# A hybrid encoder block on one core: Quarter 0's weight loads among the gate merges, T4 with the other sums, and a regrouped last quarter

## The chip, the core and the metric

The kernel runs on one core of a Trainium2 chip. Five engines matter: TensorE (PE; its weight loads are listed as PEld), VectorE (DVE), ScalarE (ACT), GpSimd (POOL) and SyncE (SP), which issues most of the DMAs. Each engine works through its own list of instructions in order and waits on semaphores. The metric is the device time of one execution in microseconds (us); less is better.

## The reference, cut to what matters

```
proj = u @ w_in                      # q, k, v of two attentions, and the gate logits
mix = (sigmoid(g_a) * (o_a @ w_branch_a) + sigmoid(g_b) * (o_b @ w_branch_b)) @ w_out
x = LN1(alpha * x + mix)
x = LN2(alpha * x + relu(x @ w_ff1)^2 @ w_ff2)      # w_ff1 1024x4096, w_ff2 4096x1024
```

There are 512 rows of 1024 columns, all in float32. Every large product is made of three matmuls on operands that were split into a rounded high part and a low remainder (line 84 makes the high part on ACT, line 85 the low part on DVE).

## The kernel before, in words

The work is laid out so that PE always has the next product. Weights of the first stages come as chunks of 512 KB (`raw`, loaded on line 126, three buffers), are split into `wh` and `wl`, and are used by `chunk()`. A tile framework puts each engine's instructions in an order of its own at build time; the engines then keep to it.

**The gate merges.** `branch(1, ...)` (line 597) makes the second branch's product in eight blocks. Each block is merged: DVE multiplies the bank by the gate (line 610), POOL adds the other branch (line 613), ACT rounds the result into `X` (line 615), DVE makes the remainder (line 616). The sixteen `G` buffers hold the gates until then.

**The output projection and LN1.** Two `s_group` loops follow (lines 916 and 934): 512 columns each, four row blocks, with the eight merged tiles against four weight chunks. The first takes its chunks as they come, the second has all four split beforehand into `V` tiles. After the second, each row block is normalised (`ln1`) and transposed on PE (line 801).

**The MLP.** Four quarters of 1024 hidden columns. `t_pair` makes the hidden tiles, ACT and DVE square and combine them. The product with a quarter of `w_ff2` is a 2x2 Strassen-Winograd scheme over row halves and column halves: seven products P1 to P7 instead of eight. Its right operands are made from four raw blocks per i (B11, B12, B22, B21, in `G` buffers of 256 KB, line 881): `sums` makes T1 = B12-B11, T3 = B22-B12, T2 = B22-T1 on DVE (line 823), and `prepare(n, i)` splits the operand of Pn. T4 is made in `prepare(6)`. B11 is loaded again after P7's operand was split, for P1, and B22 after P5's, for P3.

W and Z gather P7 and P5 over all quarters in four PSUM banks (`mm`). U gathers P1+P6 over all quarters in SBUF. `add_to` adds a bank or U to the residual rows x0 to x3 (lines 951 and 953). In the last quarter W, Z and U are added, then for b = 0 and 1 the products P4, P2 and P3 finish row blocks b+2 and b, `row_stats` (line 961) takes their statistics, and `layer_norm` (lines 728 to 742) writes them. The very last row block, 1, makes P3 in two halves of 256 columns and has a normalisation of its own, `layer_norm_last` (lines 751 to 775). Both halves of this P3 stand in one PSUM bank, `X2`:

```
X, Y, X2 = ([mm_bank()] * 2 for _ in range(3))          # line 1067
...
for lo, hi in ((0, 256), (256, S)) if b == LAST_ROW else ((0, S),):
    qt.run(3, X2, (b,), cuts=((lo, hi),))
    add_to(b, 1, X2[b][:, lo:hi], lo, hi)
    row_stats(b, 1, lo, hi)
```

Of the kernel before, what the change touches and what calls it, by code (L numbers as in the profile page):

```python
# [16 lines left out]
P = 128  # L17
# [23 lines left out]
def block_kernel(ctx, tc, w, w2, x_t, x, pos, relb, bgate, lq1, lk1, lq2, lk2, subg,  # L41
# [667 lines left out]
    for _ in branch(1, ob_h, ob_l):  # L709
        pass  # L710
# [105 lines left out]

    def sub(out, a, b):
        V.tensor_tensor(out=out, in0=a, in1=b, op=ALU.subtract)  # L823

    LEFT = {1: "A11", 2: "A12", 3: "S4", 4: "A22", 5: "S1", 6: "S2", 7: "S3"}
    lo_rows, hi_rows = slice(0, 256), slice(256, S)

    class Quarter:


        def __init__(self, q):
            self.q = q
            self.ops = {n: [None] * 4 for n in range(1, 8)}
            self.a = {}
            self.raw = [[self.load(i, r, c) for r, c in ((0, 0), (0, 1), (1, 1), (1, 0))]
                        for i in range(4)]
            self.ops[7] = [(vt(), vt()) for _ in range(4)]

        def left_tiles(self):
            for key in ("S3", "S1", "A11"):  # L840
                for i in (0, 2):
                    pair = (vt(), vt()) if key != "A11" else tuple(
                        late.tile([P, S], FR, tag="a11", bufs=4, name=name("a11"))
                        for _ in range(2))
                    for j in range(2):
                        self.a[key, i + j] = tuple(t[:, 256 * j:256 * (j + 1)] for t in pair)


        def square(self, ps):
            t = tmp_tile()  # L850
            A.activation(t, ps, AF.Relu)
            A.activation(t, t, AF.Square)
            return t

        def first(self, i):
            def f(ps):
                t = self.t0 = self.square(ps)
                sub(t[:, hi_rows], t[:, lo_rows], t[:, hi_rows])
                split(t[:, hi_rows], *self.a["S3", i])
                split(t[:, lo_rows], *self.a["A11", i])  # L860
            return f

        def second(self, i):
            def f(ps):
                t, t0, s1 = self.square(ps), self.t0, tmp_tile()[:, lo_rows]
                for left, right in (("A12", "A22"), ("S4", "S2")):
                    h, l = xt(FR), xt(FR)
                    split(t, h, l)
                    self.a[left, i] = h[:, lo_rows], l[:, lo_rows]
                    self.a[right, i] = h[:, hi_rows], l[:, hi_rows]  # L870
                    if left == "A12":
                        sub(t[:, hi_rows], t[:, hi_rows], t0[:, hi_rows])
                        V.tensor_tensor(out=s1, in0=t[:, hi_rows], in1=t0[:, lo_rows], op=ALU.add)
                        split(s1, *self.a["S1", i])
                        sub(t[:, lo_rows], t[:, lo_rows], t[:, hi_rows])
            return f


        def load(self, i, r, c, t=None):
            t = t or gt()  # L880
            nc.sync.dma_start(out=t, in_=w2[self.q, i, r, :, c * S:(c + 1) * S])
            return t

        def sums(self, i):
            b11, b12, b22, b21 = self.raw[i]
            sub(b11, b12, b11)
            sub(b12, b22, b12)
            sub(b22, b22, b11)

        def prepare(self, n, i, parts=None):  # L890

            b11, b12, b22, b21 = self.raw[i]
            src = {1: b12, 2: b21, 3: b11, 4: b22, 5: b11, 6: b22, 7: b12}[n]
            self.ops[n][i] = self.ops[n][i] or parts or (vt(), vt())
            split(src, *self.ops[n][i])
            if n == 7:
                self.load(i, 0, 0, b12)
            if n == 5:
                self.load(i, 1, 1, b11)
            if n == 6:  # L900
                sub(b22, b21, b22)

        def run(self, n, ps, blocks=(0, 1), first=True, stop=True, cuts=((0, S),)):
            jobs = [(b, lo, hi) for b in blocks for lo, hi in cuts]
            order = [(j, i) for i in range(4) for j in jobs] if n == 7 else \
                [(j, i) for j in jobs for i in range(4)]
            for (b, lo, hi), i in order:
                ah, al = (t[:, b * P:(b + 1) * P] for t in self.a[LEFT[n], i])
                wh, wl = (t[:, lo:hi] for t in self.ops[n][i])
                smm(ps[b][:, lo:hi], ah, al, wh, wl, first and i == 0, stop and i == 3)  # L910

# [3 lines left out]
    qt = None  # L915
    for n, _ in enumerate(s_group(mh, ml, evac_res(0))):
        prefetch(c0 + 5, min(c0 + 4, next_chunk[0] + 3))
        if n == 0:
            qt = Quarter(0)
        if n in (2, 4):  # L920
            for i in (n - 2, n - 1):
                qt.sums(i)
                qt.prepare(7, i)
# [39 lines left out]
    def first_pair(evacs):  # L963
        ch = [chunk() for _ in range(2)]
        ps2 = [mm_bank() for _ in range(2)]
# [13 lines left out]
    def store_row(s):  # L979
        def store(cols):  # L980
            q = A if cols.start in (S, 832) else nc.sync
            q.dma_start(out=out[s * P:(s + 1) * P, cols], in_=x1[s][:, cols])
        return store
# [3 lines left out]

    for q in range(4):
        last = q == 3
        qt.left_tiles()  # L990
# [6 lines left out]
        for i in range(4):  # L997
# [9 lines left out]
            prepare(5, (i,))  # L1007

# [7 lines left out]
        ends = dict(first=q == 0, stop=last)  # L1016
        qt.run(7, W, **ends)
        prepare(1)
        if last:
            for b in range(2):  # L1020
                add_to(b + 2, 1, W[b])
                add_to(b + 2, 0, W[b])
        qt.run(5, Z, **ends)
        prepare(6)
        if last:
            prepare(3, parts=(p3h, p3l))
            for b in range(2):
                add_to(b + 2, 1, Z[b])
                add_to(b, 1, Z[b])
# [3 lines left out]
        for b in range(2):  # L1033
            if q == 0:
                A.copy(out=U[b], in_=X[b])
            else:
                V.tensor_tensor(out=U[b], in0=U[b], in1=X[b], op=ALU.add)
            add_to(b, 0, X[b])
# [5 lines left out]
        if not last:  # L1044
# [3 lines left out]
            following = Quarter(q + 1)  # L1048
            for b in range(2):
                add_to(b, 0, X[b])  # L1050
            for i in range(4):
                following.sums(i)
                following.prepare(7, i)
# [11 lines left out]

        for b in range(2):
            X, Y, X2 = ([mm_bank()] * 2 for _ in range(3))
            for s, nh in ((b + 2, 0), (b + 2, 1), (b, 1)):
                add_to(s, nh, U[b])
            row_stats(b + 2, 1)  # L1070
            qt.run(4, X, (b,))
# [6 lines left out]
            for lo, hi in ((0, 256), (256, S)) if b == LAST_ROW else ((0, S),):  # L1078
                qt.run(3, X2, (b,), cuts=((lo, hi),))
                add_to(b, 1, X2[b][:, lo:hi], lo, hi)  # L1080
# [75 lines left out]
```

## Time and profile before

| | |
|---|---|
| median of 3 runs | 724.19 us (723.75 to 724.66) |
| the profiled execution | 725.08 us |
| its span, first to last instruction | 721.9 us |
| PE busy | 700.4 us, 97%, 3259 matmuls |
| DVE busy | 535.1 us, 74% |
| ACT busy | 382.1 us, 53% |
| POOL busy | 101.3 us, 14% |

The span is the time between the first and the last instruction of the program; 3.2 us of the profiled execution lie around it. Durations below come from this one execution. PE is at work nearly always, so a change can save time only where PE stands still or after PE's last matmul.

### The profile page before, as it was taken

What the parts mean: (1) busy time and instruction counts of PE and PEld (TensorE: products, weight loads), DVE (VectorE), ACT (ScalarE), POOL (GpSimd) and SP (SyncE); (2) the same over time, 40 slices, a digit from 0 to 9 for tenths busy, and PEclk for the clock granted to TensorE, in tenths of its full rate; (3) what the DMA queues carried; (4) which work ended last, traced back from release to release, by engine and by line L of the source; (5) the groups of instructions that cost most, each with busy time, mean ns of one, the idle gap of its engine ahead of it and who ended that gap; (6) DMA issues with size and microseconds to landing.
All of it is one profiled execution on the core that took longest, in us unless ns stands there. A gap on an engine that the chain in (4) does not pass through costs nothing.

```text
span 721.9 us, 9483 instructions
## 1 busy us (share of the span) xinstructions
PE 700.4 (97%) x3259; PEld 583.0 (81%) x3259; DVE 535.1 (74%) x1014; ACT 382.1 (53%) x698; POOL 101.3 (14%) x107
## 2 busy tenths in 40 slices
PE   9999999999999999999999999999999999999991
PEld 7888888888888888888788888888888888888881
DVE  6567668775667677759896899566984689465996
ACT  5556556645667666324366574266525674266500
POOL 2022266840121120043000000000000000000001
PEclk9999999999999999999999999999999999999996
DMA  8554233332332222376541336243451354222002
GB/s 295 197 160 127 90 85 88 103 107 73 116 109 68 67 81 88 107 277 206 197 147 65 103 125 198 94 146 117 143 178 59 124 167 160 75 88 76 12 30 87
DMA packets 36815, 87.27 MB, mean 121 GB/s; under 512 B 5664, under 2 KB 6432, under 8 KB 36768
## 3 DMA queue, kind: packets, MB, share of 16 engines
q1 hardware_dynamic: 35904, 85.56, 36.5%
q10 hardware_dynamic: 864, 1.11, 0.4%
q8 instruction: 25, 0.41, 0.2%
q14 instruction: 22, 0.18, 0.1%
HBM read 79.84 MB, written 2.10 MB: 114 GB/s over the span
## 4 chain that ended last, share of the span: by engine, by line
PE 84%; DVE 9%; ACT 2%; POOL 2%; issue 2%; DMA 0%; DVEq 0%
PE mm L184 9%; PE mm L186 9%; PE mm L185 9%; PE st L185 6%; PE st L184 6%; PE st L186 6%; PE st L189 4%; PE st L191 4%; PE st L190 4%; PE mm L189 4%; PE mm L190 4%; PE mm L191 4%; PE o L184 2%; POOL G L613 2%; PE o L185 2%; PE o L186 2%
## 5 line engine op out<-in xcount | busy, mean ns | idle before, releaser
L85 DVE TENSOR_TENSOR wl<-raw,wh 128x1024 fp32r<-128x1024 f32 (+1 forms) x86 | 105.0, 1222 | 33.2 <-ACT wh L84 33.1
L84 ACT CAST wh<-raw 128x1024 fp32r<-128x1024 f32 (+1 forms) x86 | 88.5, 1029 | 68.3 <-PE mm L185 24.1
L184 PE MATMUL mm<-X,wh 128*128 128x512 f32 x256 | 103.2, 403 | 0.0
L186 PE MATMUL mm<-X,wl 128*128 128x512 f32 x256 | 99.9, 390 | 0.0
L185 PE MATMUL mm<-X,wh 128*128 128x512 f32 x256 | 99.8, 390 | 0.0
L84 ACT CAST V<-G 128x512 fp32r<-128x512 f32 x108 | 63.7, 619 | 50.7 <-DVE G L823 25.3
L186 PE MATMUL st<-x1t,wl 128*128 128x512 f32 (+1 forms) x200 | 76.1, 381 | 0.0
L185 PE MATMUL st<-x1t,wh 128*128 128x512 f32 (+1 forms) x200 | 76.1, 381 | 0.0
L184 PE MATMUL st<-x1t,wh 128*128 128x512 f32 (+1 forms) x200 | 75.9, 381 | 0.0
L85 DVE TENSOR_TENSOR V<-G,V 128x512 fp32r<-128x512 f32 x108 | 73.8, 684 | 1.4 <-ACT V L84 1.4
L186 PEld LDWEIGHTS mm<-X,wl 128*128 128x128 f32 x256 | 48.0, 188 | 10.6
L184 PEld LDWEIGHTS mm<-X,wh 128*128 128x128 f32 x256 | 48.1, 188 | 8.8
L185 PEld LDWEIGHTS mm<-X,wh 128*128 128x128 f32 x256 | 48.2, 188 | 8.6
L285 ACT ACTIVATE e<-e,s 128x128 f32<-128x128 f32 (+3 forms) x64 | 36.0, 562 | 35.4 <-DVE s L283 34.7
L767 POOL TENSOR_SCALAR s<-s 128x1 f32<-128x1 f32 x1 | 0.4, 412 | 377.8 <-DVE s L751 377.8
L823 DVE TENSOR_TENSOR G<-G,G 128x512 f32<-128x512 f32 x64 | 46.1, 731 | 0.1
L378 POOL TENSOR_SCALAR e<-e,s 128x128 f32<-128x128 f32 (+3 forms) x32 | 36.8, 1149 | 66.3 <-DVE s L287 62.5
L191 PE MATMUL st<-V,X 128*128 128x512 f32 x116 | 45.0, 389 | 0.0
L190 PE MATMUL st<-V,X 128*128 128x512 f32 x116 | 44.9, 389 | 0.0
L189 PE MATMUL st<-V,X 128*128 128x512 f32 x116 | 44.8, 391 | 0.0
L185 PEld LDWEIGHTS st<-x1t,wh 128*128 128x128 f32 x200 | 37.6, 188 | 7.1
L186 PEld LDWEIGHTS st<-x1t,wl 128*128 128x128 f32 x200 | 37.6, 188 | 7.1
(255 smaller groups left out, 1573.5 us busy)
## 6 DMA issues: line engine op xcount, KB each, us to landing
raw<-in_w_dram SPq DMA_DIRECT2D x86, 512.0 KB
G<-in_w_dram SPq DMA_DIRECT2D x96, 256.0 KB
q<-q SPq DMA_DIRECT2D x32, 128.0 KB
G<-in_relb_dram SPq DMA_DIRECT2D x8, 256.0 KB
x<-in_x_dram SPq DMA_DIRECT2D x4, 512.0 KB
e<-in_x_t_dram SPq DMA_DIRECT2D x7, 256.0 KB
raw<-in_w_dram SPq DMA_DIRECT2D x4, 256.0 KB
out_dram<-x SPq DMA_DIRECT2D x3, 256.0 KB
```

The source lines that it names most:

```text
L84: A.copy(out=h, in_=src)
L85: i = (eng or V).tensor_tensor(out=l, in0=src, in1=h.bitcast(F32), op=ALU.subtract)
L184: T.matmul(ps, lw_h, rh, start=first, stop=False)
L185: T.matmul(ps, lw_h, rl, start=False, stop=False)
L186: T.matmul(ps, lw_l, rh, start=False, stop=last)
L189: T.matmul(ps, ah, w_h, start=first, stop=False)
L190: T.matmul(ps, ah, w_l, start=False, stop=False)
L191: T.matmul(ps, al, w_h, start=False, stop=last)
L285: A.activation(e[:, :n], e[:, :n], AF.Exp, bias=nm, scale=-1.0, accum_out=sums)
L378: G.tensor_scalar(ex[:, :n], ex[:, :n], r, None, op0=ALU.mult)
L613: G.tensor_tensor(out=m, in0=m, in1=g, op=ALU.add)
L823: V.tensor_tensor(out=out, in0=a, in1=b, op=ALU.subtract)
```

## The change

- `load_next`: the sixteen loads of Quarter 0's raw blocks are issued two at a time in the loop over `branch(1, ...)`, one pair for each merge, instead of at the first step of the first `s_group`. The other quarters load their sixteen at once, as before.
- `sums` now splits P7's operand itself and then makes T4 = B21-T2 into T3's buffer. So `prepare(7)` reloads nothing any more; B11 is loaded again after P5's split, B22 after P6's.
- Quarter 0's `sums` run at the first three steps of the first `s_group` and, for i = 3, in `first_pair`, instead of in pairs at steps 2 and 4.
- Last quarter: U of the first three quarters is added to six half rows (`flush(U)`) after the first hidden tile; P1's result is then copied to U by ACT, not added by DVE. W is no longer added by itself, but as U+W (`both`) to two half rows of each b. P1's operands are split ahead of P7 into spare `raw` and `wh` buffers. The last row's two P3 halves get a bank each. One store of the last row goes from ACT's queue to SP's.

```diff
+    qt = Quarter(0)
+    for n, _ in enumerate(branch(1, ob_h, ob_l)):
+        qt.load_next(2)
...
         def sums(self, i):
             b11, b12, b22, b21 = self.raw[i]
             sub(b11, b12, b11)
             sub(b12, b22, b12)
             sub(b22, b22, b11)
+            self.prepare(7, i)
+            sub(b12, b21, b22)
 
         def prepare(self, n, i, parts=None):
             b11, b12, b22, b21 = self.raw[i]
-            src = {1: b12, 2: b21, 3: b11, 4: b22, 5: b11, 6: b22, 7: b12}[n]
+            src = {1: b11, 2: b21, 3: b22, 4: b12, 5: b11, 6: b22, 7: b12}[n]
             self.ops[n][i] = self.ops[n][i] or parts or (vt(), vt())
             split(src, *self.ops[n][i])
-            if n == 7:
-                self.load(i, 0, 0, b12)
             if n == 5:
-                self.load(i, 1, 1, b11)
+                self.load(i, 0, 0, b11)
             if n == 6:
-                sub(b22, b21, b22)
+                self.load(i, 1, 1, b22)
...
         prefetch(c0 + 5, min(c0 + 4, next_chunk[0] + 3))
-        if n == 0:
-            qt = Quarter(0)
-        if n in (2, 4):
-            for i in (n - 2, n - 1):
-                qt.sums(i)
-                qt.prepare(7, i)
+        if n < 3:
+            qt.sums(n)
...
         ch = [chunk() for _ in range(2)]
+        qt.sums(3)
...
-            q = A if cols.start in (S, 832) else nc.sync
+            q = A if cols.start == (832 if s == LAST_ROW else S) else nc.sync
...
+    def flush(u, rows=((2, 0), (2, 1), (0, 1))):
+        for b in range(2):
+            for s, nh in rows:
+                add_to(b + s, nh, u[b])
...
             prepare(5, (i,))
+            if last and i == 0:
+                flush(U)
...
+        if last:
+            for i in range(0, 4, 2):
+                parts = [wp.tile([P, 1024], FR, tag=t, bufs=3, name=name(t))
+                         for t in (("raw", "raw"), ("raw", "wh"))[i // 2]]
+                for j in range(2):
+                    qt.prepare(1, i + j, [t[:, 512 * j:512 * (j + 1)] for t in parts])
         qt.run(7, W, **ends)
-        prepare(1)
-        if last:
-            for b in range(2):
-                add_to(b + 2, 1, W[b])
-                add_to(b + 2, 0, W[b])
+        if not last:
+            prepare(1)
...
-            if q == 0:
+            if q == 0 or last:
                 A.copy(out=U[b], in_=X[b])
...
+        both = [tmp_tile() for _ in range(2)]
         for b in range(2):
-            X, Y, X2 = ([mm_bank()] * 2 for _ in range(3))
-            for s, nh in ((b + 2, 0), (b + 2, 1), (b, 1)):
-                add_to(s, nh, U[b])
+            V.tensor_tensor(out=both[b], in0=U[b], in1=W[b], op=ALU.add)
+            for s, nh, t in ((b + 2, 0, both), (b + 2, 1, both), (b, 1, U)):
+                add_to(s, nh, t[b])
             row_stats(b + 2, 1)
+            X, Y = ([mm_bank()] * 2 for _ in range(2))
...
             for lo, hi in ((0, 256), (256, S)) if b == LAST_ROW else ((0, S),):
-                qt.run(3, X2, (b,), cuts=((lo, hi),))
-                add_to(b, 1, X2[b][:, lo:hi], lo, hi)
+                X = [mm_bank()] * 2
+                qt.run(3, X, (b,), cuts=((lo, hi),))
+                add_to(b, 1, X[b][:, lo:hi], lo, hi)
```

**How it moves instructions: the last quarter, DVE, from P6's first bank on.** `u` is U, `o` and `st` are PSUM banks, `x_2` is row block 2, `bn` its statistics, `lt` is `both`, `V` are split operands. Before:

```order
L1043 TENSOR_TENSOR u_3881<-u_3881,o_6658 128x512
L85 TENSOR_TENSOR V_6647<-G_6007,V_6646 128x512
L1043 TENSOR_TENSOR u_3882<-u_3882,st_6659 128x512
L85 TENSOR_TENSOR V_6651<-G_6015,V_6650 128x512
L951 TENSOR_TENSOR x_2_3212<-x_2_3212,u_3881 128x512
L85 TENSOR_TENSOR V_6655<-G_6023,V_6654 128x512
L951 TENSOR_TENSOR x_2_3212<-x_2_3212,u_3881 128x512
L951 TENSOR_TENSOR x_0_3210<-x_0_3210,u_3881 128x512
L961 BN_STATS bn_6692<-x_2_3212 128x6
L951 TENSOR_TENSOR x_2_3212<-x_2_3212,st_6686 128x512
```

The same place in the changed kernel:

```order
L1055 TENSOR_TENSOR u_3873<-u_3873,o_6656 128x512
L1080 TENSOR_TENSOR lt_6684<-u_3873,mm_4339 128x512
L952 TENSOR_TENSOR x_0_3210<-x_0_3210,u_3873 128x512
L952 TENSOR_TENSOR x_2_3212<-x_2_3212,lt_6684 128x512 x2
L1055 TENSOR_TENSOR u_3874<-u_3874,st_6657 128x512
L962 BN_STATS bn_6690<-x_2_3212 128x6
L1080 TENSOR_TENSOR lt_6685<-u_3874,mm_4340 128x512
L952 TENSOR_TENSOR x_1_3211<-x_1_3211,u_3874 128x512
L952 TENSOR_TENSOR x_2_3212<-x_2_3212,st_6692 128x512
L952 TENSOR_TENSOR x_3_3213<-x_3_3213,lt_6685 128x512
```

P4's operand splits (`V`) stand ahead of P6's bank now, and two sums U+W (`lt`) have come in.

**The end of the program, DVE.** `x_1` is the last row block; the bank name tells which bank a half comes from. Before:

```order
L742 SCALAR_TENSOR_TENSOR x_3_3213<-x_3_3213,s_6785,x1t_6489 128x512 x2
L951 TENSOR_TENSOR x_1_3211<-x_1_3211,st_6763 128x256
L961 BN_STATS bn_6808<-x_1_3211 128x6
L951 TENSOR_TENSOR x_1_3211<-x_1_3211,st_6763 128x256
L961 BN_STATS bn_6808<-x_1_3211 128x6
L751 BN_AGGR s_6839<-bn_6808 128x2
```

The same place in the changed kernel:

```order
L844 SCALAR_TENSOR_TENSOR x_3_3213<-x_3_3213,s_6786,x1t_6495 128x512 x2
L962 BN_STATS bn_6809<-x_1_3211 128x6 x2
L952 TENSOR_TENSOR x_1_3211<-x_1_3211,st_6812 128x256
L952 TENSOR_TENSOR x_1_3211<-x_1_3211,o_6827 128x256
L962 BN_STATS bn_6809<-x_1_3211 128x6 x2
L853 BN_AGGR s_6842<-bn_6809 128x2
```

The second half comes from bank `o` now, no longer from the bank of the first.

**The output projection, ACT, at the split of the second `s_group`'s last chunk.** `V<-raw` are the high parts of that loop's chunks, `wh<-raw` those of the first MLP chunks, `V<-G` the operand of P7. Before:

```order
L84 CAST V_3409<-raw_3445 128x512
L84 CAST V_3410<-raw_3445 128x512
L84 CAST V_3413<-raw_3447 128x512
L84 CAST wh_3681<-raw_3449 128x1024
L84 CAST V_3414<-raw_3447 128x512
L84 CAST wh_3745<-raw_3677 128x1024
```

The same place in the changed kernel:

```order
L84 CAST V_3441<-raw_3477 128x512
L84 CAST V_3442<-raw_3477 128x512
L84 CAST V_3445<-raw_3479 128x512
L84 CAST V_3446<-raw_3479 128x512
L84 CAST V_3875<-G_3408 128x512
L84 CAST wh_3673<-raw_3481 128x1024
```

The MLP chunk's cast has moved behind the last `V<-raw`.

## Rows read from the trace of the kernel before

**Rows 1.** Waits of PE: who waited for whom, us in total, times, longest.

```profile
PE st L189 <- DVE x L951: 7.9, 1, 7.9
PE mm L801 <- issue: 2.0, 1, 2.0
PE mm L190 <- DVE wl L85: 0.6, 1, 0.6
```

**Rows 2.** Windows at the end: stretch, length, busy us (instructions), PEclk, DMA share, GB/s.

```profile
core 0: us, PE busy (x) PEld busy (x) DVE busy (x) ACT busy (x) POOL busy (x), PEclk, DMA share, GB/s
...
703.20:711.20 8.00, 0.10 (x1) 0.00 (x0) 7.99 (x16) 0.29 (x1) 0.00 (x0) 0.82 0.19 71
711.20:714.20 3.00, 2.93 (x12) 2.64 (x12) 0.43 (x1) 0.00 (x0) 0.00 (x0) 0.50 0.43 159
```

**Rows 3.** Timeline, PE, last quarter: start, length, line, operation, tiles, shapes, [idle before].

```profile
685.16 0.39 PE L191 MATMUL o<-V,X 128*128 128x512 f32 x1
...
693.10 0.61 PE L191 MATMUL st<-V,X 128*128 128x512 f32 x2
...
703.02 0.28 PE L191 MATMUL st<-x1t,X 128*128 128x256 f32 x1
711.25 0.58 PE L189 MATMUL st<-x1t,X 128*128 128x256 f32 x1 [7.95 <-DVE x L951]
```

**Rows 4.** Timeline, DVE, last quarter.

```profile
666.19 2.50 DVE L85 TENSOR_TENSOR x1t<-G,x1t 128x512 fp32r<-128x512 f32 x4 [2.60 <-PE st L185]
...
688.57 0.68 DVE L1043 TENSOR_TENSOR u<-u,o 128x512 f32<-128x512 f32 x1
...
692.17 1.28 DVE L951 TENSOR_TENSOR x<-x,u 128x512 f32<-128x512 f32 x2
...
697.08 0.75 DVE L736 SCALAR_TENSOR_TENSOR x<-x,s,x1t 128x512 f32<-128x512 f32 x1
...
699.79 0.69 DVE L961 BATCH_NORM_STATS2 bn<-x 128x6 f32<-128x512 f32 x1
...
710.78 0.41 DVE L951 TENSOR_TENSOR x<-x,st 128x256 f32<-128x256 f32 x1
...
714.22 0.42 DVE L951 TENSOR_TENSOR x<-x,st 128x256 f32<-128x256 f32 x1 [2.56 <-PE st L191]
714.67 0.43 DVE L961 BATCH_NORM_STATS2 bn<-x 128x6 f32<-128x256 f32 x1
...
717.15 1.60 DVE L775 SCALAR_TENSOR_TENSOR x<-x,s,x1t 128x256 f32<-128x256 f32 x2
```

**Rows 5.** Timeline, ACT, from the second loop's chunks to LN1.

```profile
341.84 1.14 ACT L84 CAST V<-raw 128x512 fp32r<-128x512 f32 x2 [0.86 <-DMA raw<-in_w_dram]
...
350.90 1.05 ACT L84 CAST wh<-raw 128x1024 fp32r<-128x1024 f32 x1 [1.74 <-DMA raw<-in_w_dram]
```

**Rows 6.** Timeline, DVE, the same stretch.

```profile
352.50 0.69 DVE L85 TENSOR_TENSOR V<-raw,V 128x512 fp32r<-128x512 f32 x1 [2.37 <-ACT V L84]
353.11 0.68 DVE L719 SCALAR_TENSOR_TENSOR x<-x,mm 128x512 f32<-128x512 f32 x1
```

**Rows 7.** Timeline, ACT, last quarter: the first split after the last hidden tile.

```profile
667.53 0.60 ACT L84 CAST V<-G 128x512 fp32r<-128x512 f32 x1
```

**Rows 8.** Timeline, SP: the weight load that the first row of 5 waits for.

```profile
336.68 3.47 SPq L126 DMA_DIRECT2D raw<-in_w_dram  x2
```

**Rows 9.** Timeline, DVE, the gate merges.

```profile
321.87 0.69 DVE L616 SCALAR_TENSOR_TENSOR X<-G,X 128x512 fp32r<-128x512 f32 x1 [1.84 <-ACT X L615]
...
328.56 1.78 DVE L823 TENSOR_TENSOR G<-G,G 128x512 f32<-128x512 f32 x1
...
338.50 0.69 DVE L616 SCALAR_TENSOR_TENSOR X<-G,X 128x512 fp32r<-128x512 f32 x1 [0.15 <-ACT X L615]
```

**Rows 10.** Timeline, POOL, the first two gate merges.

```profile
308.00 1.29 POOL L613 TENSOR_TENSOR G<-G,G 128x512 f32<-128x512 f32 x1 [36.40 <-DVE G L610]
311.36 2.20 POOL L613 TENSOR_TENSOR G<-G,G 128x512 f32<-128x512 f32 x1 [2.07 <-DVE G L610]
```

**Rows 11.** Timeline, PE, the split of the fourth weight chunk.

```profile
343.39 0.50 PE L190 MATMUL mm<-wl,X 128*128 128x512 f32 x1 [0.62 <-DVE wl L85]
```

More of the change, by code (lines that the diff above doesn't have):

```diff
@@ L814, in x1_transposed @@
             split(fv, h, l)
[L822 to L892, printed above, removed]
-            src = {1: b12, 2: b21, 3: b11, 4: b22, 5: b11, 6: b22, 7: b12}[n]
-            self.ops[n][i] = self.ops[n][i] or parts or (vt(), vt())
-            split(src, *self.ops[n][i])
-            if n == 7:
-                self.load(i, 0, 0, b12)
-            if n == 5:
-                self.load(i, 1, 1, b11)
-            if n == 6:
-                sub(b22, b21, b22)
[L903 to L910, printed above, removed]
@@ L914, in block_kernel @@
         dest[c0 + i] = ([vt(), vt()], [vt(), vt()])
-    qt = None
     for n, _ in enumerate(s_group(mh, ml, evac_res(0))):
         prefetch(c0 + 5, min(c0 + 4, next_chunk[0] + 3))
-        if n == 0:
-            qt = Quarter(0)
-        if n in (2, 4):
-            for i in (n - 2, n - 1):
-                qt.sums(i)
-                qt.prepare(7, i)
+        if n < 3:
+            qt.sums(n)
     fin = evac_res(1)
@@ L986, in bank_pair @@
         return [mm_bank() for _ in range(2)]
+    def flush(u, rows=((2, 0), (2, 1), (0, 1))):
+        for b in range(2):
+            for s, nh in rows:
+                add_to(b + s, nh, u[b])
     for q in range(4):
         last = q == 3
+        for i in range(4):
+            qt.ops[7][i] = qt.ops[7][i] or (vt(), vt())
         qt.left_tiles()
@@ L1016, in block_kernel @@
         ends = dict(first=q == 0, stop=last)
-        qt.run(7, W, **ends)
-        prepare(1)
-        if last:
-            for b in range(2):
-                add_to(b + 2, 1, W[b])
-                add_to(b + 2, 0, W[b])
+        if last:
+            for i in range(0, 4, 2):
+                parts = [wp.tile([P, 1024], FR, tag=t, bufs=3, name=name(t))
+                         for t in (("raw", "raw"), ("raw", "wh"))[i // 2]]
+                for j in range(2):
+                    qt.prepare(1, i + j, [t[:, 512 * j:512 * (j + 1)] for t in parts])
+        qt.run(7, W, **ends)
+        if not last:
+            prepare(1)
         qt.run(5, Z, **ends)
@@ L1026, in block_kernel @@
             prepare(3, parts=(p3h, p3l))
-            for b in range(2):
-                add_to(b + 2, 1, Z[b])
-                add_to(b, 1, Z[b])
+            flush(Z, ((2, 1), (0, 1)))
         prepare(2)
@@ L1048, in block_kernel @@
             following = Quarter(q + 1)
+            following.load_next(16)
             for b in range(2):
@@ L1052, in block_kernel @@
                 following.sums(i)
-                following.prepare(7, i)
             X = bank_pair()
```

73 lines of the change are left out of this document (71 added, 2 removed).

## The prediction

> **What bounds the kernel now.** I read the waits of PE first. There are three that count [rows 1]: 7.9 us before an L189 matmul, 2.0 us before the transposes of L801, 0.6 us for a weight split. Everything else PE does back to back, and the change leaves PE's list at the same 3259 matmuls, so the answer lies in these three waits and in what follows PE's last matmul.
>
> The windows then show the longest wait from both sides: from 703.2 to 711.2 PE is busy for 0.10 us and DVE for 7.99 of 8.00 [rows 2]. The timeline tells why PE stands: the first half of the last row block's P3 ends with the matmul at 703.02, and the second half, in the same bank, starts only at 711.25, when DVE has read the first [rows 3]. DVE comes to that read at 710.78 because it is behind with everything else [rows 4]: it has had no hole worth the name since 666.19, and takes P6's first bank at 688.57 although PE ended that bank at 685.16 + 0.39 = 685.55 [rows 3]. So in the last quarter DVE is the bound. The 7.9 us of PE are a consequence of it, not a loss of their own. What the shared bank itself costs is smaller: DVE has to wait 2.56 us for the late second half [rows 4]. Its twelve matmuls take most of that, and run at a granted clock of 0.50, the 1.2 GHz level, after the idle time [rows 2]. The end is DVE's last operation, 717.15 + 1.60 = 718.75 [rows 4], and 3.15 us of stores and closing until 721.9.
>
> The two smaller waits lie around the output projection. The 2.0 us go back to LN1's statistics of the first row block, which follow the first evacuation, 353.11; DVE reached that one late because it stood idle for 2.37 us for an ACT cast [rows 6], and ACT stood because a cast of an MLP chunk, placed ahead, waited for its load [rows 5].
>
> **The last quarter, step by step.** I follow DVE's new order with durations of the old rows. A 128x512 operation is 0.68 long, but two neighbours take 1.28, so each costs 0.60 [rows 4]; a 128x256 one is 0.41 long and I charge it 0.34, with the same overlap. A normalisation of a row block is 699.79 - 697.08 = 2.71 [rows 4].
>
> First: is DVE still late at P6's bank? From the first split of P6's operands to that bank its list falls from 39 rows to 28, of which 24 are wide and 4 narrow. Gone from this stretch are four adds of W, two of U, four T4 subtractions (made with the next quarter's sums, ahead of the hidden tiles), and P1's four splits, which now stand among the hidden tiles; six adds of the old U go there too. P4's splits come in, which before lay behind the bank. 24 x 0.60 + 4 x 0.34 = 15.8 us. The first of them follows an ACT cast that ends at 667.53 + 0.60 = 668.1 [rows 7], so DVE is through at about 683.9, 1.6 us before the bank. The backlog of 3.0 us is gone and DVE now waits for PE.
>
> From 685.6 the new order is: 13 wide operations, 7.8, to 693.4, and 0.2 for an aggregate. The next add needs P2's first bank, complete at 693.10 + 0.61 = 693.71 [rows 3]: it runs from 693.75 to 694.35. A normalisation to 697.06. Five wide operations, 3.0, to 700.06; an aggregate and a wide one, 0.72, to 700.8; a normalisation to 703.5; an aggregate and an add, 0.72, to 704.2; a normalisation to 706.95. Then two narrow statistics, both half adds and the first of two closing statistics, 5 x 0.34 = 1.7, to 708.65. By then PE is long done: the second half in its own bank starts right behind 703.02 + 0.28 and is as long as the first. From the last narrow statistics to DVE's end it was 718.75 - 714.67 = 4.08 [rows 4], unchanged: 712.7. **That is 6.05 us earlier than 718.75.** I take the stores at no change; the store moved to SP's queue is issued behind one 256-column store either way.
>
> A moved step brings its loads along. P3's splits now wait for B22 loads that are issued only after P6's splits, so four reloads of 256 KB lie between them, in a DVE list that is in order. The trace shows no such load alone. Its nearest row is a weight load of 512 KB, issued at 336.68 [rows 8] and landed when its cast starts at 341.84 [rows 5]: at most 5.1 us, other loads in flight. With 5.1 for each, the four loads issued at about 668.8 to 672.5 land at 673.9 to 677.6, the last P3 split is done at about 678.9, and the 12 wide rows behind it end at 686.1, 0.5 us after the bank. Half that time costs nothing. I take 0, and keep 0.5 for the range. The Trainium skill ("DMA: Bandwidth & Descriptors", Anatomy of one DMA) gives a fixed cost of about 2.0 us and 436 GB/s; by that the estimate is 2.6 us for a reload and the cost nothing, but for the 512 KB load it gives 3.2 where the rows allow up to 5.1, so the rows set the bound.
>
> **The gate merges and the output projection, step by step.** Between the fourth merge and the first evacuation DVE's list grows by the four T4 subtractions, 4 x 0.60 = 2.4 us. Against that: the hole of 2.37 us closes, because the MLP chunk's cast now stands behind the last of the loop's own casts; and in the fourth merge a subtraction stands where DVE was idle for 1.84 us [rows 9]. Together 2.4 - 2.37 - 1.84 = -1.8 us for the evacuation, and by the same chain for LN1 and the transposes. A sum beside a running POOL add is dear, 1.78 us in place of 0.68 [rows 9]; one more such case would take 1.1 back, one saved merge wait (line 610 of the seventh merge now stands ahead of the sixth's line 616) gives about as much. PE cannot win more than 2.0 + 0.6 here [rows 1]. For the weight chunks the new place is a risk: they stand on SP behind loads that wait for merges. If a late chunk opens the hole again, the gain is 0; with one more slowed sum it is a loss of 1.1. Range +1.1 to -2.6; I take -1.6, near the sum, since each of its terms is a row. The T4 subtractions of the later quarters move by a few microseconds among the same work and I cost them at nothing: PE waited nowhere there.
>
> **The sum.** -6.05 - 1.6 = -7.6 us. The profiled execution took 725.08, so 717.5 on its footing. Its time is 0.9 above the median of 724.19; for the median I forecast **716.6**.
>
> **The rivals.**
>
> *The tail gains, the output projection does not.* For it: the weight loads of the second loop are issued behind merges now, a load took up to 5.1 us [rows 5, 8], and DVE has 2.4 us more to do there. Against it: the order puts the cast that waited behind the others. Only the tail is left, less a slowed sum: -6.05 to -4.9, a median of 718.1 to 719.3.
>
> *DVE comes late to P6's bank all the same*, as late as before, 3.0 us. The tail would keep 3.0 of its 6.05; with the 1.6 that is 719.6. It needs reloads that take about 7.5 us each in an otherwise quiet stretch. Against it: the bound of 5.1 was read in a busy one.
>
> *Slower: the merges and the sums get into each other's way.* A POOL add takes 1.29 us alone and 2.20 beside a DVE split [rows 10], and DVE pays 1.10 more for a sum [rows 9]. The new order sets 11 subtractions and 3 splits of Quarter 0 among the fourth to the last merge and the split of the fourth weight chunk, where 8 and 4 stood. The last merged tile was ready at 338.50 + 0.69 = 339.2 [rows 9], and the first matmuls on it are those around PE's small stand that began at 343.39 - 0.62 = 342.8 [rows 11], 3.6 us of room, so this decides from 3.6 us of delay on. If every one of the 14 paid 1.10, 15.4 us, PE would lose 11.8 and, with the tail's gain, the median would be 729.9. Against it: in the old order only one operation beside each add was slow, and DVE stands beside an add in about as many merges as before. The Trainium skill ("GPSIMD Engine Reference", Specifications) says that POOL shares its SBUF interfaces with VectorE and contends with DVE instructions that have two SBUF inputs; every one of these sums has, and by that rule alone this rival would be the likely one, but the rows show that the pairs which share a merge pay once.
>
> That the change does not do what it says is settled by the order: the halves have two banks, the loads stand among the merges.
>
> **How the numbers follow.** Forecast 0.75, tail only 0.16, late at P6's bank 0.06, slower 0.03. The forecast's own range goes from 724.19 - 6.05 - 2.6 = 715.5 to about 718. For eight in ten I take 715.3 to 719.3: all of the first rival, and a little below both smaller waits gone. A measurement of this kernel can tell about 0.2%, 1.45 us, from no change. The first three cases all lie beyond that: faster 0.96, the same 0.01 (a milder form of the third rival), slower 0.03.
>
> **What would show it.** Right, if the 7.9 us wait of PE is gone, the last half row runs at a granted clock of 1.00, DVE has a hole of 1 to 2 us before P6's first bank and none behind it, and its last operation ends about 8 us after PE's last matmul. The output projection is right if the transposes' wait shrinks by half or more and the 0.6 us wait goes. Wrong, if DVE waits for ACT among P3's splits, if the ACT casts of the second loop wait longer for their loads, or if a new PE wait stands at the first `s_group`.

## The result and the profile after

The changed kernel takes **716.04 us** (median of four, 715.14 to 716.55); the kernel before took 723.97 in the same comparison. The ratio is 0.9892, 95% interval 0.9873 to 0.9912: 7.9 us faster. In the session of ref_changed, below, the medians lie 9.2 us apart. The forecast was 716.6 with a range of 715.3 to 719.3. The profiled execution took 715.14, with a span of 712.9; before it was 725.08 and 721.9.

The waits of PE (who waited for whom, us in total, times, longest) answer to [rows 1]. The 7.9 and the split's 0.6 are gone, the transposes' 2.0 has become 0.7; the other two rows stood in the old list too:

```profile
PE st L294 <- DVE s L283: 1.1, 2, 0.6
PE st L250 <- DVE e L247: 1.0, 1, 1.0
PE mm L903 <- issue: 0.7, 1, 0.7
```

The windows at the end (stretch, length, busy us and instructions of PE, PEld, DVE, ACT and POOL, PEclk, DMA share, GB/s) answer to [rows 2]. PE runs without a stop and at a granted clock of 1.00 until it is done, and DVE works on alone:

```profile
699.00:702.10 3.10, 3.10 (x26) 2.88 (x24) 3.10 (x6) 0.30 (x1) 0.00 (x0) 1.00 0.32 118
702.10:710.00 7.90, 0.02 (x1) 0.00 (x0) 7.77 (x19) 0.84 (x2) 1.94 (x4) 0.65 0.28 103
```

DVE's timeline (start, length, line, operation, tiles, shapes, idle time before and its releaser) answers to [rows 4]:

```profile
665.54 0.69 DVE L85 TENSOR_TENSOR V<-G,V 128x512 fp32r<-128x512 f32 x1 [1.76 <-ACT V L84]
...
672.97 0.69 DVE L85 TENSOR_TENSOR x1t<-G,x1t 128x512 fp32r<-128x512 f32 x1 [0.45 <-ACT x1t L84]
...
682.97 0.69 DVE L1055 TENSOR_TENSOR u<-u,o 128x512 f32<-128x512 f32 x1 [0.90 <-PE o L191]
...
705.54 0.75 DVE L962 BATCH_NORM_STATS2 bn<-x 128x6 f32<-128x256 f32 x2
706.32 0.26 DVE L853 BATCH_NORM_AGGREGATE s<-bn 128x2 f32<-128x24 f32 x1
...
708.34 1.60 DVE L877 SCALAR_TENSOR_TENSOR x<-x,s,x1t 128x256 f32<-128x256 f32 x2
```

At 682.97 DVE waits for PE at P6's first bank, where before it came 3.0 us late. From there to the end it has no hole. Its last operation ends at 709.94 instead of 718.75, 8.81 us earlier. These divide as follows, each read at the same event of both traces:

| stretch | gain, us |
|---|---|
| up to the first gate merge (L616 at 309.99, now 309.25) | 0.74 |
| gate merges to the transposes (361.75, now 359.14, less 0.74) | 1.87 |
| the rest, to DVE's end (8.81 less 2.61) | 6.20 |

The first row lies ahead of everything that the change edits; the section on the hardware says what is known of it. The rest of the span, 9.0 less 8.81, is the closing.

### The profile page after: what moved, and what is told of

It reads as the page before. It is cut to its first block, busy times and chain, and to the rows that moved or that the text cites. A ratio compares the mean times of both kernels' runs of the same rounds, so it can differ in the third digit from the quotient of the medians.

```text
span 712.9 us, 9510 instructions
## 1 busy us (share of the span) xinstructions
PE 698.0 (98%) x3259; PEld 580.8 (81%) x3259; DVE 535.7 (75%) x1016; ACT 383.3 (54%) x700; POOL 100.7 (14%) x107
## 4 chain that ended last, share of the span: by engine, by line
PE 88%; DVE 5%; ACT 2%; POOL 2%; issue 1%; DMA 1%; SPq 0%; DVEq 0%
PE mm L184 9%; PE mm L186 9%; PE mm L185 9%; PE st L184 6%; PE st L186 6%; PE st L185 6%; PE st L191 4%; PE st L190 4%; PE st L189 4%; PE mm L191 4%; PE mm L190 4%; PE mm L189 4%; PE o L184 2%; PE o L185 2%; PE o L186 2%; POOL G L613 2%
## 5 line engine op out<-in xcount | busy, mean ns | idle before, releaser
L84 ACT CAST V<-G 128x512 fp32r<-128x512 f32 x104 | 61.6, 619 | 45.2 <-DVE G L716 23.5
L85 DVE TENSOR_TENSOR V<-G,V 128x512 fp32r<-128x512 f32 x104 | 71.2, 697 | 3.1 <-ACT V L84 3.1
```

The lines of the kernel that those rows point to most:

```text
L84: A.copy(out=h, in_=src)
L85: i = (eng or V).tensor_tensor(out=l, in0=src, in1=h.bitcast(F32), op=ALU.subtract)
```

## The experiments

Because of that first row the table compares traces from the first gate merge on: DVE's last end less the start of the first L616 operation. One trace each; the changed kernel profiled a second time (second row) repeats it to 0.02 us. The median and the ratio to the kernel before, taken in the same session, stand beside it. The kernel before had medians of 724.66, 724.89, 725.19 and 724.25 in the sessions of the experiments, so medians of different rows are compared by their ratios. The changed kernel's own two ratios lie 0.0021 apart, 1.5 us; only e1 lies clear of both intervals, and what the smaller steps are worth rests on the traces.

| kernel | merge to DVE's end | against changed | median | ratio, 95% interval |
|---|---|---|---|---|
| changed | 400.69 | | 716.04 | 0.9892, 0.9873 to 0.9912 |
| ref_changed (again) | 400.71 | +0.02 | 715.96 | 0.9871, 0.9854 to 0.9888 |
| before | 408.76 | +8.07 | 723.97 | 1 |
| e1_own_bank (from before) | 406.11 | +5.42 | 722.06 | 0.9958, 0.9943 to 0.9973 |
| e2_shared_bank | 403.64 | +2.95 | 718.41 | 0.9918, 0.9902 to 0.9934 |
| e3_p1_vt | 402.34 | +1.65 | 717.81 | 0.9900, 0.9881 to 0.9918 |
| e4_u_one_step | 402.04 | +1.35 | 717.90 | 0.9904, 0.9886 to 0.9921 |
| e5_loads_back | 402.68 | +1.99 | 718.41 | 0.9907, 0.9888 to 0.9926 |
| e6_t4_back | 400.93 | +0.24 | 715.79 | 0.9881, 0.9863 to 0.9900 |
| e8_sum_later | 401.61 | +0.92 | 718.02 | 0.9900, 0.9881 to 0.9918 |
| e9_rows_shared | 401.10 | +0.41 | 716.15 | 0.9879, 0.9862 to 0.9896 |
| b1_shared | 400.78 | +0.09 | 716.87 | 0.9885, 0.9867 to 0.9902 |
| b2_shared_pool | 402.01 | +1.32 | 717.71 | 0.9891, 0.9873 to 0.9908 |
| e12_no_pool | 400.55 | -0.14 | 715.81 | 0.9882, 0.9865 to 0.9898 |

### Is PE's wait of 7.95 us the loss? (e1_own_bank, e2_shared_bank)

The theory says that DVE is the bound and the wait follows from it; the rival, that the wait is the loss. The first run adds the own bank alone to the kernel before, the second takes it alone away from the changed one.

```diff
 # e1, in the kernel before
+                if lo:
+                    X2 = [mm_bank()] * 2
                 qt.run(3, X2, (b,), cuts=((lo, hi),))
 # e2, in the changed kernel
+            X = [mm_bank()] * 2
             for lo, hi in ((0, 256), (256, S)) if b == LAST_ROW else ((0, S),):
-                X = [mm_bank()] * 2
```

> The kernel before, with one edit: the second half of the last row block's P3 goes into a bank of its own; nothing else of the change. Theory (DVE is the bound of the last quarter, PE's wait of 7.95 us follows from it): PE runs the second half right behind 703.30 at a granted clock of 1.00, the wait of 7.95 is gone, and only DVE's own stand of 2.56 us and the statistics around it close. From the first half's add to the aggregate it takes 715.13 - 710.78 = 4.35 us in the kernel before and 706.32 - 704.89 = 1.43 in the changed one: 2.9 us gained, 721.1. Rival (PE's wait is the loss): 7.9 us gained, 716.1, all of the change's gain.

> The changed kernel, with the two halves of the last row block's P3 in one bank again. Theory: DVE reads the first half at 704.89 to 705.30 as now, PE stands from 700.5 to 705.3 and runs the twelve matmuls of the second half at a granted clock of 0.50, as before the change, about 2.9 us: DVE's end 2.9 us later, 718.9. If 4.8 us of idle time don't lower the clock, the twelve take 1.5 us and the end is 1.5 later, 717.5. Rival (PE's wait is the loss): all of the stand, 4.8 us later, 720.8.

In e1 the wait of 7.95 is gone from PE's list, and only 408.76 - 406.11 = 2.65 us of time with it; its transposes waited 0.2 longer, so the tail gained 2.9. DVE's timeline of e1 shows that it still comes late, now without a stand between the halves:

```profile
711.63 0.42 DVE L951 TENSOR_TENSOR x<-x,st 128x256 f32<-128x256 f32 x1
711.97 0.42 DVE L951 TENSOR_TENSOR x<-x,o 128x256 f32<-128x256 f32 x1
```

In e2 PE stands 4.7 us again, and the twelve matmuls of the second half run at a granted clock of 0.52, near the 1.2 GHz level. First its timeline, then the window of these matmuls, then DVE's timeline:

```profile
706.76 0.58 PE L189 MATMUL st<-x1t,X 128*128 128x256 f32 x1 [4.66 <-DVE x L952]
```

```profile
707.00:709.80 2.80, 2.69 (x12) 2.40 (x12) 0.24 (x2) 0.00 (x0) 0.00 (x0) 0.52 0.12 43
```

```profile
709.73 0.42 DVE L952 TENSOR_TENSOR x<-x,st 128x256 f32<-128x256 f32 x1 [2.56 <-PE st L191]
```

The cost is 2.95 us, the theory's 2.9 and not the stand's 4.7: DVE loses the 2.56 us for which it waits for the slow second half, and a little for the reordered statistics. The rival falls in both directions: 7.95 us of idle PE were worth 2.9.

### The other parts of the last quarter (e3_p1_vt, e4_u_one_step, e6_t4_back)

Each run undoes one of them: P1's splits back in the V buffers behind P7; U in one step with W's four adds; T4 of the last quarter behind P6's splits, with the old reloads.

```diff
 # e3
-        if last:
-            for i in range(0, 4, 2):
...
-                    qt.prepare(1, i + j, [t[:, 512 * j:512 * (j + 1)] for t in parts])
         qt.run(7, W, **ends)
-        if not last:
-            prepare(1)
+        prepare(1)
 # e4
-            if last and i == 0:
-                flush(U)
...
+        else:
+            flush(W, ((2, 1), (2, 0)))
...
-            if q == 0 or last:
+            if q == 0:
                 A.copy(out=U[b], in_=X[b])
...
-            V.tensor_tensor(out=both[b], in0=U[b], in1=W[b], op=ALU.add)
-            for s, nh, t in ((b + 2, 0, both), (b + 2, 1, both), (b, 1, U)):
-                add_to(s, nh, t[b])
+            for s, nh in ((b + 2, 0), (b + 2, 1), (b, 1)):
+                add_to(s, nh, U[b])
 # e6, for q == 3 alone; the second half in words
             self.prepare(7, i)
-            sub(b12, b21, b22)
+            # prepare: 7 reloads B11, 5 reloads B22, 6 is followed by
+            # sub(b22, b21, b22)
```

> The changed kernel, with P1's splits of the last quarter back in the V buffers and behind P7's matmuls, so that they leave the stretch of the hidden tiles and come into the one before P6's first bank. Theory (rows of DVE from the last hidden tile on, less its holes there): four wide rows, 2.4 us, of which the hole of 0.90 and the stand of 0.45 take 1.35: 1.05 us slower, 717.1. The T4 run has shown that a row count alone can mislead, where the rows that come in fill a stand that I had not counted (1.76 us ahead of 665.54): then no difference. Rival (what counts is the last half row's bank alone): no difference, 716.0.

> The changed kernel, with U made and added as before the change (DVE adds P1's banks to it, W is added by four rows of its own, no early adds of the old U); P1's early splits, T4 with the sums and the own bank stay. Theory: of DVE's rows from the last hidden tile on, four W adds and two adds into U come in and the two sums of U and W go out: four wide rows, 2.4 us, less the hole of 0.90 and the stand of 0.45: 1.05 us slower, 717.1. Rival (the own bank is all): no difference, 716.0.

> The changed kernel, with the T4 subtractions of the last quarter alone made behind P6's splits as before the change (old order of reloads in that quarter). Theory (rows of DVE before P6's first bank set the end, less the hole there): four wide rows, 2.4 us, come into the stretch before P6's first bank, of which the hole of 0.90 us and the stand of 0.45 us for a reload's cast take 1.3: 1.1 us slower, 717.1. Rival (only the bank and what follows PE's last matmul count): no difference, 716.0.

P1's early splits are worth 1.65 us and U's two steps 1.35, both more than the 1.05 expected; the 2.4 us of four rows less the hole of 0.90 alone would be 1.5. In each the hole at P6's first bank is gone. Counted from the transposes, DVE comes to that bank 0.80 and 0.39 us later, and the rest, 0.85 and 0.95, lies behind the bank, where two and three splits stand again. In e3 DVE stands idle where the splits had been, and then has them in its way (DVE's timeline):

```profile
667.34 0.69 DVE L85 TENSOR_TENSOR V<-G,V 128x512 fp32r<-128x512 f32 x1 [4.58 <-ACT V L84]
...
685.57 0.68 DVE L1048 TENSOR_TENSOR u<-u,o 128x512 f32<-128x512 f32 x1
```

T4 is a miss: e6 costs nothing that belongs to it. The 0.24 stand before the transposes (0.9 instead of 0.7), in work that e6 does not edit; ACT waits longer for a weight load there (first the changed kernel, then e6):

```profile
346.59 1.14 ACT L84 CAST V<-raw 128x512 fp32r<-128x512 f32 x2 [0.21 <-DMA raw<-in_w_dram]
```

```profile
347.49 1.15 ACT L84 CAST V<-raw 128x512 fp32r<-128x512 f32 x2 [0.97 <-DMA raw<-in_w_dram]
```

The tail behind the transposes is the same to 0.05 us. T4's four subtractions are back in the stretch, and P6's bank still finds DVE waiting (DVE's timeline of e6):

```profile
663.76 2.50 DVE L85 TENSOR_TENSOR x1t<-G,x1t 128x512 fp32r<-128x512 f32 x4 [1.78 <-PE st L185]
...
683.16 0.69 DVE L1067 TENSOR_TENSOR u<-u,o 128x512 f32<-128x512 f32 x1 [0.84 <-PE o L191]
```

The x1t rows are P3's four splits. In e6 they run at 663.76, as soon as their buffers are free. In the changed kernel they need a reload first and stand among the rows behind P6's splits, so DVE's list begins only at 665.54, 1.8 us later, and stands for 0.45 at 672.97: 2.2 us against the 2.4 that the four subtractions take. What T4 made early gives, its reloads take back. e6 undoes T4 in the last quarter alone; no run undoes it in the other three.

### The gate merges (e5_loads_back)

```diff
-    qt = Quarter(0)
-    for n, _ in enumerate(branch(1, ob_h, ob_l)):
-        qt.load_next(2)
+    for _ in branch(1, ob_h, ob_l):
+        pass
-        if n < 3:
-            qt.sums(n)
+        if n == 0:
+            qt = Quarter(0)
+            qt.load_next(16)
+        if n in (2, 4):
+            for i in (n - 2, n - 1):
+                qt.sums(i)
...
-        qt.sums(3)
```

> The changed kernel, with Quarter 0's blocks loaded at the first step of the output projection and its sums (T4 with them) at steps 2 and 4, as before the change; the last quarter stays changed. Theory: the stand of 0.62 us for the fourth chunk's split comes back and the one before the transposes grows from 0.66 to 2.0 us: 1.9 us slower, 717.9; with the four T4 subtractions (2.4 us) on top of the old order up to 4.3 slower, 720.3. Rival (sums beside running POOL adds cost more than they bring): 0 to 2 us faster, as 4 operations of 0.68 that take 1.77 in the changed kernel's merges would be fast.

The waits of PE in e5 are the old ones again:

```profile
PE mm L902 <- issue: 2.0, 1, 2.0
...
PE mm L190 <- DVE wl L85: 0.6, 1, 0.6
```

1.99 us slower, the lower end of the theory: the early loads and sums together are worth the two waits (no run moves one without the other), and T4's 2.4 us fit into the stand for the cast, of which e5 has this left before its first evacuation (DVE's timeline):

```profile
352.63 1.29 DVE L85 TENSOR_TENSOR V<-raw,V 128x512 fp32r<-128x512 f32 x2 [0.19 <-ACT V L84]
```

The rival, which had e5 faster, falls. Slow operations beside POOL are few in either order. DVE's timeline of the changed kernel shows them among the merges:

```profile
319.81 1.78 DVE L716 TENSOR_TENSOR G<-G,G 128x512 f32<-128x512 f32 x1
...
323.54 1.77 DVE L85 TENSOR_TENSOR V<-G,V 128x512 fp32r<-128x512 f32 x1
...
330.11 1.10 DVE L616 SCALAR_TENSOR_TENSOR X<-G,X 128x512 fp32r<-128x512 f32 x1 [1.26 <-ACT X L615]
...
334.68 1.77 DVE L716 TENSOR_TENSOR G<-G,G 128x512 f32<-128x512 f32 x1
...
350.51 0.68 DVE L821 SCALAR_TENSOR_TENSOR x<-x,mm 128x512 f32<-128x512 f32 x1
```

The four slow operations shown (the row at 350.51 is the first evacuation) are as many as from 322 to 338 before (two inside pairs of 2.39, 1.78 at 328.56 [rows 9], 1.78 at 336.57) and as in e5.

**The sum of the parts.** Undone one by one they cost 2.95 + 1.65 + 1.35 + 0.24 + 1.99 = 8.18 us; the kernel before costs 8.07. That the two agree so closely is in part luck: the 0.24 is not T4's, e3 and e4 both use up the same hole of 0.90, and T4 in the first three quarters and the store on SP's queue are undone by no run.

### Attempts at a faster one (e8_sum_later, e9_rows_shared, b1_shared, b2_shared_pool, e12_no_pool)

DVE alone has 8 us of work behind PE's last matmul, so three runs (e9, b1, b2) give part of it to ACT and POOL; two (e8 and again b2) work on the 0.7 us before the transposes; e12 takes POOL's help away. ref_changed is the changed kernel once more.

```diff
 # e8: the third block group's sums behind LN1
-        if n < 3:
+        if n < 2:
             qt.sums(n)
...
+        qt.sums(2)
         qt.sums(3)
 # e9 and b1: second halves of rows 2, 0 and 3, here for rows 2 and 0
+            A.activation(y[:, hi], y[:, hi], AF.Identity, bias=nmr, scale=rs)
+            G.tensor_tensor(out=y[:, hi], in0=y[:, hi], in1=g[1], op=ALU.mult)
+        G.tensor_tensor(out=y[:, hi], in0=y[:, hi], in1=b[1], op=ALU.add)
 # b2: b1, and
+    on_pool.add(c0 + 3)
 # e12: the last normalisation's columns from 832 on made by DVE
```

> A version that might beat both: the changed kernel, with the second halves of the normalisations of row blocks 2, 0 and 3 given to ACT (one activation) and POOL (two operations), as the last row block's end already is. Theory (DVE is the bound from P6's first bank to the end): six rows of 0.66, 4.0 us, leave DVE; the end is then bound by PE's last matmul, about 702.2, and the 709.94 - 705.21 = 4.7 us that follow the last half add: 707.0 instead of 709.94, 2.9 us faster, 713.1. Rival (each POOL operation slows the DVE operation beside it by 1.1 us, as in the gate merges): 6 x 1.1 = 6.6 us come back, 2.6 slower, 718.6; if only DVE operations with two inputs in SBUF are slowed, at most three or four of them, about no difference.

> The changed kernel with second halves of normalisations given away in another manner than in the run before: for row blocks 2 and 0 ACT scales and POOL multiplies and adds, the bias of it computed on DVE; for row block 3 ACT scales and POOL only adds; all these stores are issued by SP, so that no store waits on ACT's queue ahead of a square root. Theory (in the run before, DVE's stands of 1.42, 0.59 and 0.20 us for square roots, held up on ACT behind a store that waited for POOL, and a slowed operation of 1.20 ate the gain): DVE saves 2 x (1.32 - 0.21) + 0.66 = 2.9 us, pays about 0.25 for each of some four operations beside POOL, 1.9 us faster, 714.1. Rival (POOL's traffic and not the queue ate the gain): no difference, 716.0, the operations of DVE beside POOL taking as long as the time that they save.

> The changed kernel, with its last 192 columns of the last normalisation, which ACT and POOL make, given back to DVE. It asks whether POOL's help in the kernel as it stands brings anything: DVE's last two operations (256 and 320 columns) take 1.60 us together, with POOL's two of 0.60 and 0.65 beside them, where two of this form alone take about 0.95. Theory (POOL takes from DVE about what it takes over): DVE does some 0.5 us more work and gets 0.65 back; end within 0.2 us of 709.94 counted from the first merge, time the same, 716.0. Rival (POOL's work is free): 0.5 us later, 716.5.

> The changed kernel, with the sums of Quarter 0's third block group (four subtractions and a split, 5 x 0.60 = 3.0 us of DVE) moved from the output projection's third step to the place of the fourth's, behind LN1. Theory (DVE is late at the first evacuation, 350.51, and with it PE at the transposes): the remaining stand of 0.66 us before the transposes goes, 0.7 us faster, 715.4. Rival (the evacuation then waits for the casts of weight chunks, ahead of which ACT stood 1.96 and 1.20 us for loads): no difference, 716.0.

> The one before, and the two low halves of the last MLP chunk that is split during the output projection made by POOL instead of DVE: two operations of 0.60 us less on DVE ahead of the first evacuation. Theory: the stand of 0.66 us before the transposes goes, 0.7 us faster than the run before, 713.4. Rival (POOL slows the subtractions beside it by 1.1 us each, as in the gate merges): the stand grows by up to 1.0 us, 715.1.

> The changed kernel itself, on the same chip as the next two, so that they can be compared with it in one session: 716.0, or 8 us less than the kernel before. The executions so far start their second microsecond stretch of work between 25.8 and 27.7 us after the span's start, whatever the kernel; if that scatter is the chip's and not the kernels', this one shows it too, and the last quarter measured from the first merge is the same to 0.1 us.

None is faster beyond the measurement. ref_changed did not show the scatter of the start that it was to look for: its first merge starts at 309.24, as in the first trace. In e9 the last aggregate came 0.97 us earlier, but square roots were stuck on ACT behind stores that waited for POOL (1.42 us of DVE's time in one place), and the end was 0.41 later. b1 removed that, and stayed at +0.09. Its DVE timeline, and then POOL's, tell why:

```profile
693.91 0.75 DVE L844 SCALAR_TENSOR_TENSOR x<-x,s,x1t 128x512 f32<-128x512 f32 x1
...
696.63 1.28 DVE L992 BATCH_NORM_STATS2 bn<-x 128x6 f32<-128x512 f32 x2
...
698.19 1.44 DVE L844 SCALAR_TENSOR_TENSOR x<-x,s,x1t 128x512 f32<-128x512 f32 x1
...
703.18 1.71 DVE L844 SCALAR_TENSOR_TENSOR x<-x,s,x1t 128x512 f32<-128x512 f32 x1
...
705.41 1.15 DVE L859 SCALAR_TENSOR_TENSOR x<-x,s,x1t 128x512 f32<-128x512 f32 x1
```

```profile
696.42 1.30 POOL L852 TENSOR_TENSOR x<-x,x1t 128x512 f32<-128x512 f32 x1 [358.35 <-ACT x L851]
697.80 1.29 POOL L858 TENSOR_TENSOR x<-x,x1t 128x512 f32<-128x512 f32 x1
...
702.72 3.29 POOL L858 TENSOR_TENSOR x<-x,x1t 128x512 f32<-128x512 f32 x2
```

The normalising operations beside POOL take 1.44, 1.23, 1.71 and 1.15 where they take 0.74 alone: 2.6 us back, of 2.9 saved; a further 0.4, which makes the +0.09, I have not traced. The statistics beside POOL at 696.63 keep their length, and so does an add from PSUM at 704.81 (0.68). How much longer a row gets can be read off: the one at 698.19 ends at 698.19 + 1.44 = 699.63, POOL's operation at 697.80 + 1.29 = 699.09; the one at 705.41 ends at 706.56, POOL's pair at 706.01. Each of the four, and each of the slow operations among the merges, before and after, ends 0.54 to 0.56 us after POOL's operation beside it. So in these traces DVE pays the rest of POOL's operation, once. The Trainium skill ("SBUF — State Buffer", SBUF: two separate sides) says that a POOL operation that reads SBUF and a DVE operation with two inputs in SBUF, or in a 2-port mode, shut each other out for the whole instruction. These rows agree for the first kind, the lengthened ones having two such inputs and the statistics one; none here tests the second. e12 shows the same give and take in the kernel as it stands, by DVE's last three operations:

```profile
710.13 1.27 DVE L869 SCALAR_TENSOR_TENSOR x<-x,s,x1t 128x256 f32<-128x256 f32 x3
```

Three operations without POOL end 0.14 us sooner than two beside it: POOL's 192 columns bring nothing.

e8 did not put DVE's rows where the code did: the sums still ran ahead of the first evacuation, two short stands for casts came in, and the transposes waited 1.6 us. b2's two POOL subtractions (of the second loop's last weight chunk; the expectation calls it an MLP chunk) made PE wait 1.9 us for LN1 there, with DVE's two rows beside them at 0.85 and 1.67. In the other three attempts the wait stayed at 0.6 to 0.7 us.

## Why the prediction was right, and where not

**What bounds.** Right: e1 and e2 show from both sides that DVE sets the end and that the shared bank itself cost little. I had named its 2.56 us; it is 2.9 with the statistics that are packed more closely.

**The tail, -6.05.** Measured -6.20. The walk behind P6's bank held: from the bank's end, 685.55, to the start of the last statistics, 708.65, it gave 23.1 us; from the bank's arrival at 682.97 to 705.54 + 0.75/2 it is 22.9. The closing stretch of 4.08 is unchanged.

**The backlog before P6's bank.** Right in sign, the room was mis-sized: I had DVE through 1.6 us before the bank, and it was 0.9, just below the 1 to 2 that I had named as a sign. Nothing of the end hangs on the difference. The reload that I took at 0 with 0.5 in the range cost DVE a stand of 0.45, hidden in that hole. The two loads that ACT waited for were issued on SP at 667.93 and 669.20 and landed at 670.95 and 672.32, 3.0 and 3.1 us, well under the bound of 5.1. They are nearer to the estimate of 2.6 worked out from the Trainium skill ("DMA: Bandwidth & Descriptors", Anatomy of one DMA), but that section gives its figures for transfers issued by GpSimd, and these were issued by SP.

**The step that failed** is the list of what goes out of the stretch: "four T4 subtractions", 2.4 us, stood there as part of the gain. e6 shows that part to be nothing. The 39 rows that I counted from the first split of P6's operands include P3's four splits; in the kernel before these run from 666.19 on [rows 4], ahead of that split, from which only 35 rows are left to the bank:

```profile
668.61 0.68 DVE L85 TENSOR_TENSOR V<-G,V 128x512 fp32r<-128x512 f32 x1
```

So T4's four rows go out and P3's four come in. The reload that comes with T4's new place keeps P3's splits from filling the stand ahead of the list, which begins later by nearly as much as the four rows took. The row count gave the right sum, since it counted the changed kernel's whole list of 28, but it laid the gain on the wrong edit: it belongs to the bank (2.9), P1 (1.65) and U (1.35).

**The gate merges, -1.6.** Measured -1.87, by e5 1.99, within the range of -2.6 to +1.1: the first evacuation came 1.86 us earlier (the sum said 1.8), the split's wait went, the transposes' shrank by 1.3. The terms held less well than the total. From the first merge to the evacuation DVE's idle time fell by 3.3 us and not by 2.37 + 1.84 = 4.2, mostly because a new hole of 1.26 stands at 330.11; its work grew by 1.5 and not by 2.4, mostly because the slow operation behind that hole costs 0.7 less than the others. That the two differences cancel is luck.

**The signs of being wrong.** Two of those that I had named came: DVE waits for ACT among P3's splits (the 0.45), and ACT's casts of the second loop wait longer for their loads, where the longest such wait before was 0.86 [rows 5] (ACT's timeline of the changed kernel):

```profile
338.32 0.62 ACT L84 CAST V<-raw 128x512 fp32r<-128x512 f32 x1 [1.76 <-DMA raw<-in_w_dram]
...
342.90 1.14 ACT L84 CAST V<-raw 128x512 fp32r<-128x512 f32 x2 [1.96 <-DMA raw<-in_w_dram]
...
345.24 1.14 ACT L84 CAST V<-raw 128x512 fp32r<-128x512 f32 x2 [1.20 <-DMA raw<-in_w_dram]
```

Neither cost time: DVE has a hole of 0.90 behind the first, and none between 337 and the evacuation at 350.51 from the second. They were signs of less room, not of a wrong sum.

**The rivals.** The tail alone: ruled out by the transposes and by e5. Late at P6's bank: ruled out by the hole of 0.90. The merges and sums in each other's way: four slow operations before and after. The mechanism that I priced is real, as b1 shows, but in the merges it decides nothing, for the reason given there: a pair that shares a merge pays once. Of the three splits that this rival counts to Quarter 0, one is of a weight chunk.

**The total.** 6.05 + 1.6 made 7.6 and the traces show 8.07 from the first merge on; the medians 7.9 and, in the other session, 9.2.

## What to carry to other kernels

A long wait of the busiest engine can be a consequence: price it by what the engine that it waits for would do with the time, here 2.9 of 7.95 us. When rows are moved out of a full stretch, ask also when the stretch can begin; a step whose reload comes late gives back what it saves. And work given to POOL beside DVE operations with two SBUF inputs is not free: 2.9 us of DVE's work given away came back as 2.6 of longer rows. In these traces it cost DVE nothing only beside rows of another kind, the statistics and an add from PSUM.

## What was not expected of the hardware

The executions start differently, in work that no edit touches. PE's first matmuls of 512 columns take 0.63 us each and start 0.43 apart; later ones take 0.39 and start 0.23 apart. That this is the clock is inferred from the lengths and not shown: the view of windows gives a granted clock of 1.00 for the stretch from 4 to 8 us in both traces below. What speaks for it are P3's matmuls of 256 columns. They start 0.21 us apart at the granted clock of 0.50, the 1.2 GHz level (the kernel before [rows 2]), and 0.12 apart at 1.00, the 2.4 GHz level (the changed kernel), about the same times per column. The change came at about 5.7 us in both executions of the changed kernel and in e6, at 8.5 in the kernel before and at 10.4 in e3, with PE at matmuls of the first projection each time. PE's timeline, first of the changed kernel, then of e3:

```profile
5.75 0.47 PE L190 MATMUL mm<-wl,X 128*128 128x512 f32 x1
6.05 0.39 PE L191 MATMUL mm<-wh,X 128*128 128x512 f32 x1
```

```profile
10.00 0.63 PE L191 MATMUL mm<-wh,X 128*128 128x512 f32 x1
10.43 0.51 PE L189 MATMUL mm<-wh,X 128*128 128x512 f32 x1
10.78 0.39 PE L190 MATMUL mm<-wl,X 128*128 128x512 f32 x1
```

The first merge then starts at 309.25 and at 311.05, 1.8 us apart, and the kernel before stands between them with 309.99. The changed kernel, e6 (309.19) and e3 have the same code up to the last quarter, so no edit ahead of the first merge makes the difference. Whether it is chance from execution to execution or goes with the program as a whole stays open; one profile of each, and the changed kernel alike in two, don't decide it. The times of one kernel spread by 0.8 to 3.6 us (before: 722.8 to 726.4 in one session), so for an edit worth 1 us a trace counted from a common event tells more than the medians.
